# Second block: 11 of 31 convolution taps of four blocks move to the tensor engine

## The chip, the cores and the metric

One core of a Trainium2 chip runs the whole program: TensorE (PE, matrix products), VectorE (DVE), ScalarE (ACT), GpSimd (POOL) and SyncE (SP, which issues the DMAs). The metric is the device time of one execution in microseconds (us); lower is better.

## The reference

Three blocks follow each other on x of 1024 positions by 1024 columns, all in float32. The change touches only the second, and of it only the mixers:

```python
h = rmsnorm(x, norm_mix_g[l])
p = h @ w_in[l]
p_rwkv = p[..., :D_RWKV_IN]
p_rwkv = p_rwkv + (token_shift(p_rwkv) - p_rwkv) * shift_mu[l]
p_conv = p[..., D_RWKV_IN:]
y_rwkv = rwkv7_group(p_rwkv, ...)
y_conv = conformer_conv_group(p_conv, ...)
x = x + jnp.concatenate([y_rwkv, y_conv], axis=-1) @ w_out[l]
```

`conformer_conv_group` makes h = a * sigmoid(b) of two halves of 512 columns, then a causal depthwise convolution along time with 31 taps (each channel has its own 31 weights and a bias), a layer norm over the channels and a SiLU:

```python
h = u[..., :D_CONV] * jax.nn.sigmoid(u[..., D_CONV:])
h = lax.conv_general_dilated(h, conv_w, window_strides=(1,), padding=[(30, 0)], feature_group_count=D_CONV) + conv_b
```

`rwkv7_group` runs, for 8 heads of 64, a state update over time (S is 64 by 64 for each head), then a norm per head, a bonus and a gate:

```python
sa = jnp.einsum('bhvk,bhk->bhv', S, a_t)
S = S * w_t[:, :, None, :] + sa[..., :, None] * b_t[:, :, None, :] + v_t[..., :, None] * k_t[:, :, None, :]
y = jnp.einsum('bhvk,bhk->bhv', S, r_t)
```

## The kernel before

`mixers_2` does all this. Time is cut into two halves of 512 positions (`hf` 0 and 1) and the recurrence into eight units `u` of 128 positions (four a half), each of two chunks `c` of 64.

**Projections.** Every projection of 128 columns for one half is 24 matmuls of 128x128 by 128x512 (each f32 product is three products of high and low halves, L1152 to L1154), cut into eight *parts* of three. `shift_mix` and `rwkv_proj` project for the recurrence (12 a half, P[hf]) and store to DRAM; `rwkv_lora` (L[hf]) has two more. `conv_project` makes block i of the convolution for one half (C[j] with i = j % 4, hf = j // 4): generator `one` projects the gate and takes its tanh into `cvh`, `two` projects the value and multiplies. Then channels lie on partitions and time along the row, so that a tap is `h[:, j:j+512]` times one column of weights.

**Taps.** Tap 0 with the bias starts `cva` on ACT (L1496). Of the other 30, 10 are `other`: ACT multiplies into `cp` (L1500, two buffers) and POOL adds it to `cva` (L1501). 20 are `own`: DVE multiplies and adds into `cvp` (L1506, L1509), which lies in PSUM with one buffer (`cv`). A last DVE instruction adds `cvp` to `cva` (L1516). These 31 entries per block go to a list `taps`.

**The recurrence** of a unit has four generators, cut by `yield d` where d is the planner's waiting time: `rwkv_keys` (decays, normed keys), `rwkv_scores` (score matrices L1307, inverse of a triangular matrix in `chunk_inverse` by repeated products L1434 and L1441 with DVE between, L1325 and L1323 for the bonus), `rwkv_chain` (the state z through both chunks: L1352 and L1354 with z, correction rh on DVE, L1359, then `uv` copied from PSUM by DVE and ACT, L1361 and L1362, then L1365 and L1367, and z = (pc + z) * gl in two DVE instructions, L1370 and L1371) and `rwkv_post` (norm, transposes L1401, gate L1396, L1404 to L1407; result to DRAM `mixd`, for unit 7 straight into the tiles `mts1`).

**The order of the work.** PE keeps the order in which the program emits its instructions; the other engines' orders are made by the framework's scheduler from the dependences. `drive` emits: it has a clock of its own in planner units. A step of a generator costs STEP = 0.9 and is ready when its waiting time has passed; ready steps go first (chain, post, scores, keys). Otherwise one part of the list `work` is fed, which costs PART = 0.7, as long as fewer than SPARE + DENSE * steps (40 + 1.6 a step) have been fed; otherwise the clock moves by 0.25 with nothing emitted. After each turn taps are taken from the list, one for every TAP = 1.6 units. Eight units have 25 steps each.

`work` holds in order C[0], P[0], C[1], C[2], C[3], a reload with a wait of 16 units, L[1], P[1] with the norm N[0] beside it, C[4] to C[7], the load of the mixed tiles of the first half once four posts are done, a wait of 12, the first half's output projection O[0] to O[3] (64 parts, L1620 to L1622, through the small tile `xo`, two buffers, loaded at L1613 and stored at L1627) with N[1] beside it, the join of N[1], and after seven posts `mixed1` (mixed tiles of the second half), a wait of 12, and O[4] to O[7]. "Beside" means that one piece of the norm is emitted per SIDE = 4 parts; the join emits the rest, one per 2.5 units. `conv_norm` (N[hf]) first empties the taps' list, four per piece, then has two transposes (L1533) and four output pieces (L1547 to L1553, tile `cu`, stored to `mixd`) for each quarter. Ahead of `drive`, 14 projections are fed with a tap per two parts.

Of the kernel before, what the change touches and what calls it, by code (L numbers as in the profile page):

```python
# [23 lines left out]
NPART = 8  # L24
EARLY = 16
OTHER = 10
# [2 lines left out]
PART = 0.7  # L29
LOAD = 4.0  # L30
TAP = 1.6
SPARE = 40
DENSE = 1.6


# [9 lines left out]
class Kern:  # L45
# [1293 lines left out]
    def rwkv_chain(self, st, z, pool, psum):  # L1339


        nc = self.nc
        ar, sb, bkt, uv, yf, w1, gl, bon = st
        hps = [slice(0, 64), slice(64, 128)]
        pairs = [(b, h, hp) for b in range(4) for h, hp in enumerate(hps)]
        of = lambda t, c: t.rearrange("p (b c) d -> p b c d", b=4)[:, :, c]

        yp = psum.tile([128, 2, 4, 64], F32, tag="y", name="yp")
        for c in range(2):
            pc = psum.tile([128, 2, 4, 64], F32, tag="ch", name="pc")  # L1350
# [11 lines left out]
            nc.scalar.copy(uvc[64:128, :, c, 1], pc[64:128, 1])  # L1362
            yield 1.8
            for b, h, hp in pairs:
                nc.tensor.matmul(pc[hp, 0, b], lhsT=bkt[:, h, 2 * b + c], rhs=uv[:, 2 * b + c, h], start=True, stop=True)  # L1365
            for b, h, hp in pairs:
                nc.tensor.matmul(yp[hp, c, b], lhsT=sb[:, h, 2 * b + c], rhs=uv[:, 2 * b + c, h], start=False,  # L1367
                                 stop=(c == 1 and b == 3))
# [12 lines left out]
    def rwkv_post(self, q, y, st, bon, sgd, lg, pool, psum):  # L1381
# [16 lines left out]
        for b in range(4):  # L1398
            for c in range(2):
                for hp in (slice(0, 64), slice(64, 128)):  # L1400
                    nc.tensor.matmul(ps[hp, b, c], lhsT=y[hp, 4 * c + b], rhs=self.ident[hp, hp], start=True, stop=True)  # L1401
        o = pool.tile([128, 4, 128], F32, tag="mst", name="mst", bufs=1)
        for b in range(4):
            nc.scalar.activation(out=o[:, b], in_=ps[:, b].rearrange("p c t -> p (c t)"), func=ACT.Identity,  # L1404
                                 scale=c2["ln_g"][:, b:b + 1], bias=c2["ln_b"][:, b:b + 1])
# [61 lines left out]
            nc.scalar.copy(yf[qs[2 * h], :, 32:64], ps[qs[2 * h]])  # L1467
        return yf

    def conv_project(self, i, hf, xts, pool, psum, accs, taps):  # L1470


        nc = self.nc
        w = self.a["w_in_2"][0]
        cw, cb = self.c2["conv_w"], self.c2["conv_b"]
        keep = {}

        def one():
            hl = yield (w, 2304 + i * 128)
            h = keep[0] = pool.tile([128, 542], F32, tag="cvh", name="cvh", bufs=2)  # L1480
            nc.gpsimd.tensor_copy(h[:, 0:30], self.halo[:, i])
            ps = psum.tile([128, 512], F32, tag="mm", name="mps")
            yield from self.parts(ps, hl, xts[hf])
            nc.scalar.activation(out=h[:, 30:542], in_=ps, func=ACT.Tanh, scale=0.5)

        def two():
            hl = yield (w, 1792 + i * 128)
            h = keep[0]
            v = h[:, 30:542]
            ps = psum.tile([128, 512], F32, tag="mm", name="mps")  # L1490
            yield from self.parts(ps, hl, xts[hf])
            nc.vector.scalar_tensor_tensor(out=v, in0=v, scalar=1.0, in1=ps, op0=ALU.add, op1=ALU.mult)
            if hf == 0:
                nc.gpsimd.tensor_copy(self.halo[:, i], h[:, 512:542])
            acc = pool.tile([128, 512], F32, tag="cva", name="cva", bufs=4)
            nc.scalar.activation(out=acc, in_=h[:, 0:512], func=ACT.Identity, scale=cw[:, i:i + 1], bias=cb[:, i:i + 1])  # L1496
            accs.append(acc)
            def other(j):
                t = pool.tile([128, 512], F32, tag="cy", name="cp", bufs=2)
                nc.scalar.activation(out=t, in_=h[:, j:j + 512], func=ACT.Copy, scale=cw[:, 4 * j + i:4 * j + i + 1])  # L1500
                nc.gpsimd.tensor_tensor(out=acc, in0=acc, in1=t, op=ALU.add)  # L1501

            def own(j):
                x, c = h[:, j:j + 512], cw[:, 4 * j + i:4 * j + i + 1]
                if 1 in keep:
                    nc.vector.scalar_tensor_tensor(out=keep[1], in0=x, scalar=c, in1=keep[1], op0=ALU.mult, op1=ALU.add)  # L1506
                else:
                    keep[1] = psum.tile([128, 512], F32, tag="cv", name="cvp")
                    nc.vector.tensor_scalar(out=keep[1], in0=x, scalar1=c, scalar2=None, op0=ALU.mult)  # L1509

            done = 0
            for j in range(1, 31):
                mine = done < j * OTHER // 30
                done += mine
                taps.append(lambda f=other if mine else own, j=j: f(j))
            taps.append(lambda: nc.vector.tensor_tensor(out=acc, in0=acc, in1=keep[1], op=ALU.add))  # L1516
        return [one(), two()]

    def conv_norm(self, accs, taps, hf, store, pool, psum):
# [36 lines left out]
    def mixers_2(self, xt0, psum, late, es):  # L1556
# [13 lines left out]
        states, taps = {}, []  # L1570
        accs, loras, done = [[], []], [{}, {}], []
        def reload():
            yield None
# [27 lines left out]
        def out_part(hf, c0):  # L1601
# [6 lines left out]
            for t in range(4):  # L1608
                ps = psum.tile([128, 512], F32, tag="mm", name="mps")[:, :256]
                if hf == 0:  # L1610
                    x = lo.tile([128, 256], F32, tag="xo", name="xo", bufs=2)
                    xr = self.xd[t * 128:(t + 1) * 128, c0:c0 + 256]
                    nc.sync.dma_start(out=x, in_=xr)  # L1613
                else:
                    x = xs1[t][:, c0:c0 + 256]
# [95 lines left out]
        def scores(u):  # L1711
            states[u] = yield from self.rwkv_scores(states[u], r, psum, lambda: freed.append(u))

        def drive():

            running, begun = {}, {"keys": 0, "scores": 0, "chain": 0}
            tapped, fed, steps = 0.0, 0, 0

            def step(name):
                nonlocal steps
# [14 lines left out]
            def ready(name):  # L1737
                if name not in running or running[name][1] > clock[0]:
                    return False

                return name != "keys" or running[name][2] < 2 or len(freed) >= begun["keys"]
            while begun["chain"] < 8 or running:
                a, b, c = [begun[n] for n in ("keys", "scores", "chain")]
# [15 lines left out]
                    fed += 1  # L1759
                else:  # L1760
                    clock[0] += 0.25
                while tapped < clock[0] and taps:
                    taps.pop(0)()
                    tapped = max(tapped, clock[0] - 3 * TAP) + TAP

        more(EARLY)
        late(lambda: more(4 * NPART - EARLY))
# [17 lines left out]
        z = [r.tile([128, 4, 64], F32, tag="z", name="z", bufs=3)]  # L1785
        nc.gpsimd.memset(z[0], 0.0)

        C = [self.conv_project(j % 4, j // 4, xts, cv, psum, accs[j // 4], taps) for j in range(8)]
        N = [self.conv_norm(accs[hf], taps, hf, store, cv, psum) for hf in range(2)]
        O = [out_part(i // 4, 256 * (i % 4)) for i in range(8)]  # L1790
        work += C[0] + P[0][4:8] + C[1] + P[0][8:] + C[2] + C[3] + [reload(), ("wait", 16)] + L[1]
        work += [("beside", N[0])] + P[1] + [("join",)] + C[4] + C[5] + C[6] + C[7]
        work += [("when", lambda: len(posts) >= 4), mixed(), ("wait", 12), ("beside", N[1])] + O[:4]
        work += [("join",), ("when", lambda: len(posts) >= 7), mixed1(), ("wait", 12)] + O[4:]
        for i in range(14 * NPART):
            more(1)
            if i % 2 and taps:
                taps.pop(0)()
        with tc.manual_schedule(engines={mybir.EngineType.PE}):
            drive()  # L1800
            for part in feeder:
                clock[0] += PART if part else 0.25
        es.close()
        self.open_xtb("left")
        return mts1, xs1
# [492 lines left out]
```

## Time and profile before

| what | value |
|---|---|
| median of 3 runs | 3507.09 us (3503.11 to 3510.9) |
| the profiled execution | 3508.77 us |
| its span | 3507.1 us |
| TensorE's mean granted clock | 0.964 |

The span is what the trace covers; the execution's own time holds 1.7 us more around it. Positions are us from the span's start; the second block's mixers lie at about 1440 to 2162. A group's row gives line, engine, operation, output and inputs, shapes and count, then busy time, mean duration in ns, and idle time of the engine just before with what ended it. A matmul's duration overlaps the next one's, so the distance between starts tells PE's rate. In a list of waits the waiting instruction stands first, then whom it waited for, the total in us, how often, and the longest.

### The profile page before, as it was taken

How to read it: one execution, taken by the hardware profiler on the slowest of the kernel's cores; microseconds unless marked ns; L12 is line 12 of the kernel's file. 1: busy time of each engine (PE TensorE's matmuls, PEld its weight loads, DVE VectorE, ACT ScalarE, POOL GpSimd, SP SyncE). 2: the span in 40 equal slices, each digit the busy share in tenths (PEclk: the TensorE clock that was granted, in tenths of full speed). 3: DMA queues.
4: the chain of work that ended last, by engine and by line, in shares of the span. 5: the costliest groups of instructions: out<-in, count | busy, mean ns of one | idle time of the engine just before them, and what ended most of it. 6: DMA issues, size and time to landing. Idle time of an engine off the chain costs nothing.

```text
span 3507.1 us, 54368 instructions
## 1 busy us (share of the span) xinstructions
PE 3284.1 (94%) x22362; PEld 2664.9 (76%) x22362; DVE 2143.6 (61%) x3018; ACT 1166.5 (33%) x2259; POOL 1510.8 (43%) x1233
## 2 busy tenths in 40 slices
PE   8999898989999999996988788999999999998998
PEld 5877787867888888885766677888888887776877
DVE  7656787767766766758548753544443343687684
ACT  2322221232222222445546544211111143443561
POOL 3455653584434434576326524433333343344120
PEclk9999999999999999997998888999999999999999
DMA  5210035211111111452231224322221121111132
GB/s 194 73 53 25 25 106 180 75 47 49 48 42 50 47 48 48 149 167 94 67 93 50 72 93 143 102 72 73 66 69 47 51 84 37 43 34 40 43 109 78
DMA packets 276789, 261.97 MB, mean 75 GB/s; under 512 B 10178, under 2 KB 219694, under 8 KB 276538
## 3 DMA queue, kind: packets, MB, share of 16 engines
q1 hardware_dynamic: 276540, 258.48, 22.9%
q8 instruction: 176, 2.88, 0.3%
q14 instruction: 73, 0.60, 0.1%
HBM read 225.66 MB, written 32.78 MB: 74 GB/s over the span
## 4 chain that ended last, share of the span: by engine, by line
PE 38%; DVE 6%; issue 2%; POOL 2%; ACT 2%; DMA 2%; SPq 0%; POOLq 0%; DVEq 0%; ACTq 0%
PE mps L178 7%; PE mps L180 6%; PE mps L179 6%; PE dps L178 3%; PE dps L180 3%; PE dps L179 3%; DVE cvp L1506 1%; PE yp L2032 1%; PE tps L2023 1%; POOL hl L133 1%; PE mps L1152 1%; PE mps L1620 1%; DVE om L2013 1%; PE mps L1621 0%; PE mps L1622 0%
## 5 line engine op out<-in xcount | busy, mean ns | idle before, releaser
L133 POOL TENSOR_TENSOR hl<-raw,hl 128x1024 fp32r<-128x1024 f32 x249 | 629.9, 2531 | 869.3 <-ACT hl L132 661.5
L178 PE MATMUL mps<-xt,hl 128*128 128x512 f32 x1888 | 756.0, 401 | 12.7 <-DVE cacc L944 7.8
L180 PE MATMUL mps<-xt,hl 128*128 128x512 f32 x1888 | 746.2, 396 | 0.0
L179 PE MATMUL mps<-xt,hl 128*128 128x512 f32 x1888 | 746.2, 395 | 0.0
L132 ACT CAST hl<-raw 128x1024 fp32r<-128x1024 f32 x262 | 274.6, 1049 | 610.8 <-PE dps L180 441.5
L178 PEld LDWEIGHTS mps<-xt,hl 128*128 128x128 f32 x1888 | 359.6, 191 | 94.5 <-DVE cacc L944 8.2
L180 PEld LDWEIGHTS mps<-xt,hl 128*128 128x128 f32 x1888 | 358.8, 190 | 79.4 <-issue 0.9
L179 PEld LDWEIGHTS mps<-xt,hl 128*128 128x128 f32 x1888 | 359.4, 190 | 75.1 <-issue 1.0
L931 DVE SCALAR_TENSOR_TENSOR cacc<-apad,cols,cacc 128x1024 f32<-128x1024 f32 x176 | 345.0, 1964 | 112.7 <-ACT cacc L925 102.1
L178 PE MATMUL dps<-hl,hid 128*128 128x512 f32 x832 | 327.2, 393 | 2.6 <-DVE x L960 2.6
L180 PE MATMUL dps<-hl,hid 128*128 128x512 f32 x832 | 326.7, 393 | 0.6 <-POOL hid L853 0.6
L179 PE MATMUL dps<-hl,hid 128*128 128x512 f32 x832 | 326.7, 393 | 0.0
L1854 DVE TENSOR_TENSOR x<-x,dps 128x512 f32<-128x512 f32 x224 | 152.7, 687 | 171.6 <-PE dps L180 171.5
L178 PEld LDWEIGHTS dps<-hl,hid 128*128 128x128 f32 x832 | 156.6, 188 | 38.2 <-DVE x L960 3.0
L180 PEld LDWEIGHTS dps<-hl,hid 128*128 128x128 f32 x832 | 156.4, 188 | 35.9 <-POOL hid L853 1.1
L179 PEld LDWEIGHTS dps<-hl,hid 128*128 128x128 f32 x832 | 156.6, 188 | 34.5
L1841 DVE TENSOR_TENSOR ftmp<-ftmp 128x512 f32<-128x512 f32 x64 | 60.6, 949 | 177.1 <-ACT ftmp L1840 177.1
L1152 PE MATMUL mps<-xt,hl 128*128 128x512 f32 x352 | 154.4, 439 | 4.2 <-ACT cs L1552 4.2
L178 PE MATMUL mps<-hl,xt 128*128 128x512 f32 (+1 forms) x368 | 137.7, 377 | 6.1 <-ACT xt L244 1.7
L1153 PE MATMUL mps<-xt,hl 128*128 128x512 f32 x352 | 142.5, 405 | 0.0
L1154 PE MATMUL mps<-xt,hl 128*128 128x512 f32 x352 | 142.5, 405 | 0.0
L179 PE MATMUL mps<-hl,xt 128*128 128x512 f32 (+1 forms) x368 | 137.2, 374 | 1.6 <-DVE hl L133 1.3
(518 smaller groups left out, 6238.1 us busy)
## 6 DMA issues: line engine op xcount, KB each, us to landing
raw<-in_w_in_dram SPq DMA_DIRECT2D x108, 512.0 KB
raw<-in_w_ff_dram SPq DMA_DIRECT2D x64, 512.0 KB
raw<-in_ffn_up_dram SPq DMA_DIRECT2D x44, 512.0 KB
raw<-in_w_out_dram SPq DMA_DIRECT2D x36, 512.0 KB
adar<-in_ada_w_dram SPq DMA_DIRECT2D x32, 512.0 KB
adar<-in_w_ada_dram SPq DMA_DIRECT2D x48, 256.0 KB
raw<-in_ffn_down_dram SPq DMA_DIRECT2D x22, 512.0 KB
xd<-x SPq DMA_DIRECT2D x16, 512.0 KB
```

The costliest lines, as they stand in the source:

```text
L132: nc.scalar.copy(hl[:, 0], raw)
L133: (low or nc.gpsimd).tensor_tensor(out=hl[:, 1], in0=raw, in1=f32(hl[:, 0]), op=ALU.subtract)
L178: self.nc.tensor.matmul(ps, lhsT=sh, rhs=mh, start=(i == 0), stop=False)
L179: self.nc.tensor.matmul(ps, lhsT=sh, rhs=ml, start=False, stop=False)
L180: self.nc.tensor.matmul(ps, lhsT=sl, rhs=mh, start=False, stop=(i == n - 1))
L931: nc.vector.scalar_tensor_tensor(out=acc, in0=pad[:, i // 3:i // 3 + 16, i % 3:i % 3 + 64], scalar=cw[:, i * 22 + j:i * 22 + j + 1], in1=a ...
L1152: nc.tensor.matmul(ps, lhsT=sh, rhs=xt[k][:, 0], start=(k == 0), stop=False)
L1153: nc.tensor.matmul(ps, lhsT=sh, rhs=xt[k][:, 1], start=False, stop=False)
L1154: nc.tensor.matmul(ps, lhsT=sl, rhs=xt[k][:, 0], start=False, stop=(k == 7))
L1506: nc.vector.scalar_tensor_tensor(out=keep[1], in0=x, scalar=c, in1=keep[1], op0=ALU.mult, op1=ALU.add)
L1841: nc.vector.tensor_tensor(out=v, in0=v, in1=v, op=ALU.mult)
L1854: nc.vector.tensor_tensor(out=xs[t][:, c], in0=xs[t][:, c], in1=ps, op=ALU.add)
```

## The change

For the second half's blocks (C[4] to C[7], `diagonal` true), taps 0 to 10 go to PE: ACT scales the identity by one column of weights (`dg`, three buffers), and a matmul with this diagonal adds the shifted row into PSUM, 11 matmuls a block in plain f32, emitted as further parts of the generator behind two yields. ACT then makes `cva` from that PSUM tile and the bias. Taps 11 to 30 stay on DVE. The first half keeps 10 taps on ACT and POOL, in a new order. In the chain, both `uv` copies go to ACT, ACT scales the old state ahead of time (`zg`), and four DVE instructions finish the state. The norm no longer empties the taps' list but waits until all blocks are summed; taps are also handed out at the same pace behind `drive`, and one per part ahead of it. The last post waits for the mixed tiles. SPARE is 60, `xo` has one buffer, and the post's output shares y's buffer.

```diff
-SPARE = 40
+SPARE = 60
...
-            nc.vector.tensor_copy(uvc[0:64, :, c, 0], pc[0:64, 1])
-            nc.scalar.copy(uvc[64:128, :, c, 1], pc[64:128, 1])
+            for h, hp in enumerate(hps):
+                nc.scalar.copy(uvc[hp, :, c, h], pc[hp, 1])
+            zg = pool.tile([128, 4, 64], F32, tag="zg", name="zg", bufs=1)
+            for b in range(4):
+                nc.scalar.activation(out=zg[:, b], in_=z[:, b], func=ACT.Copy, scale=gl[:, 2 * b + c:2 * b + c + 1])
...
-            nc.vector.tensor_tensor(out=zn, in0=pc[:, 0], in1=z, op=ALU.add)
-            nc.vector.tensor_tensor(out=zn, in0=zn, in1=of(gl[:, :, None], c).to_broadcast([128, 4, 64]), op=ALU.mult)
+            for b in range(4):
+                nc.vector.scalar_tensor_tensor(out=zn[:, b], in0=pc[:, 0, b], scalar=gl[:, 2 * b + c:2 * b + c + 1], in1=zg[:, b],
+                                               op0=ALU.mult, op1=ALU.add)
...
-        o = pool.tile([128, 4, 128], F32, tag="mst", name="mst", bufs=1)
+        o = pool.tile([128, 4, 128], F32, tag="y", name="mst", bufs=1)
...
+            if diagonal:
+                yield
+                yield
+                diags = []
+
+                def diag(j):
+                    diags.append(pool.tile([128, 128], F32, tag="dg", name="dg", bufs=3))
+                    nc.scalar.activation(out=diags[j], in_=self.ident, func=ACT.Copy, scale=col(j))
+                diag(0)
+                diag(1)
+                ps = psum.tile([128, 512], F32, tag="mm", name="tps")
+                for j in range(OTHER + 1):
+                    if j + 2 <= OTHER:
+                        diag(j + 2)
+                    nc.tensor.matmul(ps, lhsT=diags[j], rhs=h[:, j:j + 512], start=(j == 0), stop=(j == OTHER))
+                    if j < OTHER:
+                        yield
+            acc = pool.tile([128, 512], F32, tag="cva", name="cva", bufs=4)
+            if diagonal:
+                nc.scalar.activation(out=acc, in_=ps, func=ACT.Identity, bias=cb[:, i:i + 1])
+                mine = []
+            else:
+                nc.scalar.activation(out=acc, in_=h[:, 0:512], func=ACT.Identity, scale=col(0), bias=cb[:, i:i + 1])
+                mine = [lambda j=j: other(j) for j in range(1, OTHER + 1)]
+            accs.append(acc)
+            for j in range(OTHER + 1, 31):
+                taps.append(lambda j=j: own(j))
+                if mine and j % 2:
+                    taps.append(mine.pop(0))
+            taps.extend(mine + [total])
...
-        while taps:
-            for _ in range(min(len(taps), 4)):
-                taps.pop(0)()
+        while len(summed) < 4 * (hf + 1):
             yield
...
-                    x = lo.tile([128, 256], F32, tag="xo", name="xo", bufs=2)
+                    x = lo.tile([128, 256], F32, tag="xo", name="xo", bufs=1)
...
+        def tap():
+            while tapped[0] < clock[0] and taps:
+                taps.pop(0)()
+                tapped[0] = max(tapped[0], clock[0] - 3 * TAP) + TAP
...
+                if name == "post" and begun["chain"] == 8 and len(mts1) < 8:
+                    return False
...
-        for i in range(14 * NPART):
+        while len(done) < 12:
             more(1)
-            if i % 2 and taps:
+            if taps:
                 taps.pop(0)()
         with tc.manual_schedule(engines={mybir.EngineType.PE}):
             drive()
             for part in feeder:
                 clock[0] += PART if part else 0.25
+                tap()
```

`own(j)` is as before; `total` is the last DVE instruction of a block, and appends the block to `summed`.

More of the change, by code (lines that the diff above doesn't have):

```diff
@@ L1468, in chunk_inverse, with conv_project @@
         return yf
-    def conv_project(self, i, hf, xts, pool, psum, accs, taps):
+    def conv_project(self, i, hf, xts, pool, psum, accs, taps, summed, diagonal):
         nc = self.nc
@@ L1494, in two, with own @@
                 nc.gpsimd.tensor_copy(self.halo[:, i], h[:, 512:542])
-            acc = pool.tile([128, 512], F32, tag="cva", name="cva", bufs=4)
-            nc.scalar.activation(out=acc, in_=h[:, 0:512], func=ACT.Identity, scale=cw[:, i:i + 1], bias=cb[:, i:i + 1])
-            accs.append(acc)
+            col = lambda j: cw[:, 4 * j + i:4 * j + i + 1]
+            def own(j):
+                x = h[:, j:j + 512]
+                if 1 in keep:
+                    nc.vector.scalar_tensor_tensor(out=keep[1], in0=x, scalar=col(j), in1=keep[1], op0=ALU.mult, op1=ALU.add)
+                else:
+                    keep[1] = psum.tile([128, 512], F32, tag="cv", name="cvp")
+                    nc.vector.tensor_scalar(out=keep[1], in0=x, scalar1=col(j), scalar2=None, op0=ALU.mult)
@@ L1498, in other @@
             def other(j):
                 t = pool.tile([128, 512], F32, tag="cy", name="cp", bufs=2)
-                nc.scalar.activation(out=t, in_=h[:, j:j + 512], func=ACT.Copy, scale=cw[:, 4 * j + i:4 * j + i + 1])
+                nc.scalar.activation(out=t, in_=h[:, j:j + 512], func=ACT.Copy, scale=col(j))
                 nc.gpsimd.tensor_tensor(out=acc, in0=acc, in1=t, op=ALU.add)
[L1503 to L1516, printed above, removed]
+            def total():
+                nc.vector.tensor_tensor(out=acc, in0=acc, in1=keep[1], op=ALU.add)
+                summed.append(i)
+            if diagonal:
[14 more added lines that the diff above has]
+                        yield
@@ new lines, in two @@
+            acc = pool.tile([128, 512], F32, tag="cva", name="cva", bufs=4)
+            if diagonal:
+                nc.scalar.activation(out=acc, in_=ps, func=ACT.Identity, bias=cb[:, i:i + 1])
+                mine = []
+            else:
+                nc.scalar.activation(out=acc, in_=h[:, 0:512], func=ACT.Identity, scale=col(0), bias=cb[:, i:i + 1])
[5 more added lines that the diff above has]
+                    taps.append(mine.pop(0))
@@ L1517, in conv_project, with conv_norm @@
+            taps.extend(mine + [total])
         return [one(), two()]
-    def conv_norm(self, accs, taps, hf, store, pool, psum):
+    def conv_norm(self, accs, summed, hf, store, pool, psum):
         nc, c2 = self.nc, self.c2
-        while taps:
-            for _ in range(min(len(taps), 4)):
-                taps.pop(0)()
+        while len(summed) < 4 * (hf + 1):
             yield
@@ L1568, in store @@
             nc.sync.dma_start(out=mixd[k * 128:(k + 1) * 128, hf * 512 + q * 256:hf * 512 + q * 256 + 256], in_=m)
-        states, taps = {}, []
+        states, taps, summed = {}, [], []
         accs, loras, done = [[], []], [{}, {}], []
@@ L1712, in scores @@
             states[u] = yield from self.rwkv_scores(states[u], r, psum, lambda: freed.append(u))
+        tapped = [0.0]
+        def tap():
+            while tapped[0] < clock[0] and taps:
+                taps.pop(0)()
+                tapped[0] = max(tapped[0], clock[0] - 3 * TAP) + TAP
         def drive():
             running, begun = {}, {"keys": 0, "scores": 0, "chain": 0}
-            tapped, fed, steps = 0.0, 0, 0
+            fed, steps = 0, 0
             def step(name):
@@ L1761, in drive @@
                     clock[0] += 0.25
-                while tapped < clock[0] and taps:
-                    taps.pop(0)()
-                    tapped = max(tapped, clock[0] - 3 * TAP) + TAP
+                tap()
         more(EARLY)
@@ L1786, in mixers_2 @@
         nc.gpsimd.memset(z[0], 0.0)
-        C = [self.conv_project(j % 4, j // 4, xts, cv, psum, accs[j // 4], taps) for j in range(8)]
-        N = [self.conv_norm(accs[hf], taps, hf, store, cv, psum) for hf in range(2)]
+        C = [self.conv_project(j % 4, j // 4, xts, cv, psum, accs[j // 4], taps, summed, j > 3) for j in range(8)]
+        N = [self.conv_norm(accs[hf], summed, hf, store, cv, psum) for hf in range(2)]
         O = [out_part(i // 4, 256 * (i % 4)) for i in range(8)]
@@ L1802, in mixers_2 @@
                 clock[0] += PART if part else 0.25
+                tap()
         es.close()
```

## The prediction

> **What bounds the kernel now.** I read the page first, then the second block's stretch by windows, then its waits, then single lines.
>
> ```profile
> span 3507.1 us, 54368 instructions
> PE 3284.1 (94%) x22362; PEld 2664.9 (76%) x22362; DVE 2143.6 (61%) x3018; ACT 1166.5 (33%) x2259; POOL 1510.8 (43%) x1233
> ```
>
> TensorE (PE) bounds the kernel as a whole (94%), so work that is added to it must find holes. The holes are in the stretch where the four edited convolution blocks lie. The columns: stretch and its length, busy time and instruction count of PE, weight loads, DVE, ACT and POOL, then the granted clock.
>
> ```profile
> 1843.00:1986.00 143.00, 108.22 (x1843) 86.26 (x1843) 118.93 (x198) 84.92 (x207) 97.12 (x76) 0.79 0.19 59
> 1986.00:2036.00 50.00, 47.77 (x1064) 43.16 (x1060) 27.75 (x58) 21.46 (x66) 15.89 (x11) 1.00 0.28 90
> 2036.00:2080.00 44.00, 41.12 (x1006) 36.15 (x1006) 25.37 (x55) 19.61 (x62) 14.43 (x13) 0.98 0.30 95
> 2080.00:2120.00 40.00, 21.69 (x239) 17.73 (x238) 15.12 (x31) 19.68 (x68) 12.11 (x17) 0.59 0.40 139
> ```
>
> Call these A, B, C and T. A begins where the second projection of C[4] ends; B, C and T where the chains of units 5, 6 and 7 begin. In A, PE stands idle for 143 - 108.2 = 34.8 us, and at a clock of 0.79 it loses about 108.2 x 0.21 = 22.7 us more: 57 us of slack. DVE is 83% busy there and POOL 68%. B and C are nearly full. T has 18.3 us of idleness and some 9 us (21.69 x 0.41) of slow clock. Whom PE waits for in A (total us, times, longest):
>
> ```profile
> PE ps L1441 <- DVE iq L1436: 10.5, 5, 6.0
> PE ps L1434 <- DVE ix L1443: 7.1, 3, 3.0
> PE ps L1396 <- DVE bon L1325: 4.4, 1, 4.4
> PE pc L1365 <- ACT uv L1362: 4.2, 1, 4.2
> ```
>
> These are steps of the recurrence; their DVE results come late because taps stand before them in DVE's queue. The taps by line (busy us, mean ns), over both halves, and then the first and the last DVE instruction of the second half's four blocks:
>
> ```profile
> L1506 DVE SCALAR_TENSOR_TENSOR cvp<-cvh,cols,cvp 128x512 f32<-128x512 f32 x152 | 113.9, 749 | 3.1
> L1501 POOL TENSOR_TENSOR cva<-cva,cp 128x512 f32<-128x512 f32 x80 | 106.7, 1333 | 7.3 <-ACT cp L1500 4.4
> L1500 ACT ACTIVATE cp<-cvh,cols 128x512 f32<-128x512 f32 x80 | 56.0, 719 | 27.7 <-POOL cva L1501 27.7
> ```
> ```profile
> 1842.32 0.74 DVE L1509 TENSOR_SCALAR cvp<-cvh,cols 128x512 f32<-128x512 f32 x1
> ...
> 1977.08 0.69 DVE L1516 TENSOR_TENSOR cva<-cva,cvp 128x512 f32<-128x512 f32 x1 [3.47 <-POOL cva L1501]
> ```
>
> In these 135 us the planner's clock passes about 78 units (57 parts of 0.7, some 42 steps of 0.9), enough to hand out 49 entries of the taps' list at one per 1.6 units. All 124 (31 a block) ran: DVE, ACT and POOL take taps as soon as their data exist, and only PE keeps the written order. So A holds 80 DVE taps and 40 of ACT and POOL.
>
> **The change part by part.**
>
> *Diagonal matmuls, added to PE:* 4 x 11 = 44, of 128x128 by 128x512 in plain f32. L1323 has that form; the other two rows are the same matmul of two neighbouring projection parts.
>
> ```profile
> 1668.04 1.13 PE L1323 MATMUL ps<-a,b 128*128 128x512 f32 x2
> 1669.00 0.60 PE L1263 MATMUL ps<-ident,rb 128*128 128x128 f32 x4
> ```
> ```profile
> 1561.48 0.39 PE L1152 MATMUL mps<-xt,hl 128*128 128x512 f32 x1
> 1562.16 0.39 PE L1152 MATMUL mps<-xt,hl 128*128 128x512 f32 x1
> ```
>
> What follows L1323 starts 0.96 us after it: 44 x 0.96 = +42 us of PE. A projection part (three matmuls, split into high and low halves) takes 0.68, so 0.227 a matmul, and the lower bound is 44 x 0.227 = 10 us. I take 0.96, from the row with the same operand type. By the Trainium skill ("TensorE: Matmul & The Clock Gate", Back-to-back issue gap) a matmul of 512 columns takes 518 warm cycles, about 216 ns, with no word of the type; by that the 44 would be an estimated 9.5 us. The projections agree with it and the f32 row (0.96 us) doesn't.
>
> *ACT and POOL taps of the four blocks, removed:* 40 x 1.333 = 53 us of POOL and 40 x 0.719 = 29 us of ACT go, and 44 diagonals come to ACT, 128x128 like L1230 (quoted below): 44 x 0.396 = 17 us. Neither engine sets the end, so by itself this is zero; its worth is in A's waits.
>
> *DVE taps:* the same 80, but spread. C[5]'s can't start before C[4]'s sum (one "cv" buffer), nor that before C[4]'s diagonals, and C[5]'s projections stand behind those in PE's order. By the slots counted next, C[4]'s, C[5]'s and a good half of C[6]'s taps stay in A; some 28 (28 x 0.749 = 21 us) move to B.
>
> *Part slots.* Behind A's start, before has 48 projection parts and 64 output parts. After has 96 (84 for three blocks of 16 projection parts, one empty part and 11 diagonals, and 12 for C[4]), the mixed load, then the 64. How many slots the planner opens hangs on its constants, not on the work. Before used 57 in A (48 + 18/2) and lost about 9 to the 12-unit wait behind C[7]; B and C by L1620 alone, two per part, a few records missing:
>
> ```profile
> 1843.00:1986.00 143.00, 5.39 (x18) 3.42 (x18) 0.79 0.19 59
> 1986.00:2036.00 50.00, 20.94 (x68) 12.86 (x68) 1.00 0.28 90
> 2036.00:2080.00 44.00, 13.60 (x43) 7.91 (x42) 0.98 0.30 95
> ```
>
> So after gets A 66, B about 36, C about 30 (its end was empty), unit 7's chain about 13, less 8 for the wait, which now falls into C: 137 of 161. Some 22 to 24 output parts are left when the last chain ends, where before had none. I use 22.
>
> *The stages.* Four output parts take 3.06 us:
>
> ```profile
> 2029.54 0.38 PE L1620 MATMUL mps<-hl,xt 128*128 128x256 f32 x1
> ...
> 2032.60 0.69 PE L1465 MATMUL ps<-yf,iq 32*32 32x32 f32 x32
> ```
>
> A: PE gets 33 diagonals (+32), loses 16 projection parts (-11) and 9 output parts at 0.77 (-7): +14 us of work into 57 us of slack. If the slack goes with the taps, 28 of 80 take 20 us of it along; for the 40 POOL adds and their ACT halves I let another 14 go. That is 14 - 34 = -20, between +8 (only 6 us of slack goes) and -40 (all but 3 goes). B: equal work, but 21 us of taps on a DVE that was busy 27.75 of 50: +5 (0 to 12). C: output parts to its end: +4. Unit 7's chain: 13 x 0.77 = 10 us of parts in a sparsely filled 13 us: +3.
>
> *The tail.* The last post waits for the mixed tiles, and these for all output parts and the end of the norm N[1]:
>
> ```profile
> 2092.86 0.64 PE L1367 MATMUL yp<-uv,sb 128*64 128x64 f32 x16
> ```
> ```profile
> 2099.01 0.43 DVE L1553 SCALAR_TENSOR_TENSOR cu<-cs,cu 128x256 f32<-128x256 f32 x1 [0.63 <-ACT cs L1552]
> ...
> 2103.27 0.43 DVE L1553 SCALAR_TENSOR_TENSOR cu<-cs,cu 128x256 f32<-128x256 f32 x1 [1.07 <-ACT cs L1552]
> ```
> ```profile
> 2103.73 1.90 DMA mixd<-cu
> ...
> 2107.03 7.43 DMA xt<-mixd
> ```
> ```profile
> SPq L1613 <- DMA xd<-xo: 26.0, 14, 3.2
> ```
>
> Before, unit 7's last matmuls end at 2093.5 and the mixed tiles have landed at 2114.5: 21 us. After: 22 x 0.77 = 17 us of parts; about four pieces of N[1], which advances one piece per four parts and starts late, at 4.26 us each (2103.27 - 2099.01): 17; from the last store to the landing 2114.5 - 2103.7 = 10.7. That is 45, so +24 (+7 if N[1] keeps pace). The single "xo" buffer lets each load wait for the store just ahead of it in SP's queue, 26.0 / 14 = 1.9 us, beside a load of like length: some 4.5 us per tile against 3.06 of PE, and behind the load in SP's queue stand weight loads. Five tiles are bare: 0 to +7, I take +2. Tail: +26.
>
> *At nothing.*
>
> ```profile
> L1230 ACT ACTIVATE sq<-ink,cols 128x128 f32<-128x128 f32 x32 | 10.2, 396 | 6.5 <-DMA ink<-rkvd 6.5
> ...
> L1266 DVE SCALAR_TENSOR_TENSOR kk<-ink,cols,ps 128x128 f32<-128x128 f32 x32 | 8.9, 338 | 4.0 <-PE ps L1263 3.9
> ```
>
> The state step's two DVE instructions become four of half L1266's size, so at most 4 x 0.338 = 1.4 us per half chunk, even if the removed two cost nothing; the gain is bounded by the 4.2 us that PE waited for uv, which stand in A's slack. Parts cover all but unit 7's two steps, and now those too; bare, two would cost under 3 us. The scaled states lie on ACT behind uv, during PE's work. "mst" in y's slot: the next y waits for a store (1.90 us) but comes eight planner units later; uncovered, 7 x 1.9 = 13 us. SPARE: by C[4], 32 + 1 + 16 + 96 = 145 parts are fed against a limit of 40 + 1.6 x 100 steps = 200; it never binds. The quicker hand-out of taps ahead of the drive and the even pace after it: taps run on their data, so zero, at most 5 us either way.
>
> Sum: -20 + 5 + 4 + 3 + 26 = **+18 us** on the profiled execution's 3508.77 (span 3507.1 and 1.7 around it): 3526.8. The median of the runs lies 1.7 lower, so **3525 us**, with 3515 to 3537 as this case's own range.
>
> **The rivals.** (1) *A recovers whole: faster.* POOL may delay DVE directly, not only through queues:
>
> ```profile
> L1281 DVE SCALAR_TENSOR_TENSOR a<-inr,cols,a x32: 336/342/2451, 1589.8 to 2010.1; 128x128 f32<-128x128 f32 x32
> ```
>
> One such instruction took 2.45 us against a median of 0.34. If the POOL adds cause most of A's waits, A gives -40 and B nothing: -40 + 0 + 4 + 3 + 23 = -10, 3497 us. It decides once A shortens by more than 37 us. Against it: C[4]'s 20 DVE taps stay in their place, and the longest waits name DVE. The Trainium skill ("SBUF — State Buffer", Who interferes with whom) says that a DVE instruction with two SBUF inputs contends with a GpSimd one that reads SBUF; the long L1281 agrees. Chance 0.25. (2) *Even:* A -32, tail +20, the rest as above: 3507 us, 0.15. (3) *ACT tied to PE: slower still.* With three "dg" buffers, 32 of the builds wait in ACT's queue for a matmul, with uv, y and the casts behind them; at 0.6 us of each on the path +19, 3544 us. For it: ACT lost 27.7 us in the same way to POOL (L1500's row). 0.13. (4) *The f32 matmuls go at the projections' rate:* 10 us for 42, 3493 us; L1323 speaks against it. 0.02. My forecast: 0.45.
>
> **How the numbers follow.** A difference of 0.2%, 7 us, is about what a measurement can tell from none. Slower 0.45 + 0.13 = 0.58, same 0.15, faster 0.25 + 0.02 = 0.27. The range reaches over (1) to (3): 3494 to 3546.
>
> **What would show it.** Diagonal matmuls 0.9 to 1 us apart; A's taps spread into B, A's clock near 0.9, the chain of unit 5 about 20 us earlier; output parts and N[1]'s pieces behind unit 7's chain, and the mixed tiles landing 10 to 25 us later. As many DVE waits in A as now, or no output parts behind unit 7, would prove the step concerned wrong.

## The result, and the profile after

The changed kernel takes 3530.48 us (median of 4 runs, 3526.86 to 3535.31), beside 3508.65 us for the kernel before. The ratio is 1.0065 with a 95% interval of 1.0046 to 1.0085: slower by 0.65%, where 3525 us was forecast. The profiled execution took 3533.67 us, against 3508.77 before. Its page, the span and the engines' busy time:

```profile
span 3532.0 us, 54607 instructions
PE 3315.4 (94%) x22450; PEld 2669.5 (76%) x22450; DVE 2133.0 (60%) x3034; ACT 1176.8 (33%) x2343; POOL 1455.9 (41%) x1193
```

The span grew by 24.9 us. PE is busy 31 us longer and POOL 55 us shorter. The forecast's stages A, B, C and the end, cut in the changed kernel's windows at the places that match (columns as before: PE, weight loads, DVE, ACT, POOL, then the granted clock):

```profile
1846.00:1960.00 114.00, 104.27 (x1806) 69.11 (x1806) 89.22 (x167) 68.03 (x204) 37.38 (x31) 0.96 0.15 44
1960.00:2015.00 55.00, 48.61 (x927) 32.52 (x928) 42.58 (x81) 30.05 (x92) 17.59 (x13) 0.91 0.20 64
2015.00:2068.00 53.00, 48.67 (x1096) 43.91 (x1091) 25.35 (x60) 22.33 (x74) 10.97 (x12) 1.00 0.20 62
2068.00:2108.00 40.00, 33.07 (x361) 30.75 (x358) 13.36 (x31) 15.68 (x56) 11.95 (x12) 0.96 0.37 116
2108.00:2141.00 33.00, 9.09 (x62) 6.62 (x60) 7.65 (x12) 8.16 (x19) 10.08 (x9) 0.62 0.54 181
```

A is full: PE is busy 104 of 114 us at a clock of 0.96, where before it was busy 108 of 143 at 0.79. B's DVE went from 27.75 to 42.58 us: the taps that moved. The last window is the price: for 33 us PE does 9 us of work. The starts of the chains of units 5, 6 and 7, unit 7's last matmuls, the matmul with which the second half's output parts have had their last long wait, and the first matmul behind the last of them, which marks the end of the mixers:

```profile
1960.24 0.68 PE L1352 MATMUL pc<-z,ar 64*64 64x64 f32 x16
...
2015.27 0.68 PE L1352 MATMUL pc<-z,ar 64*64 64x64 f32 x16
...
2067.80 0.68 PE L1352 MATMUL pc<-z,ar 64*64 64x64 f32 x16
...
2085.59 0.64 PE L1370 MATMUL yp<-uv,sb 128*64 128x64 f32 x16
...
2140.88 0.58 PE L1650 MATMUL mps<-hl,xt 128*128 128x256 f32 x1 [8.67 <-ACT xt L861]
...
2185.74 1.47 PE L237 MATMUL tps<-ident,xhat 128*128 128x128 f32 x12
```

The same rows in the kernel before (unit 7's last matmuls, at 2092.86, are shown above the result):

```profile
1985.61 0.68 PE L1352 MATMUL pc<-z,ar 64*64 64x64 f32 x16
...
2036.28 0.68 PE L1352 MATMUL pc<-z,ar 64*64 64x64 f32 x16
...
2080.38 1.12 PE L1352 MATMUL pc<-z,ar 64*64 64x64 f32 x16
...
2119.98 0.58 PE L1622 MATMUL mps<-hl,xt 128*128 128x256 f32 x1 [1.59 <-POOL xt L862]
...
2161.97 1.91 PE L237 MATMUL tps<-ident,xhat 128*128 128x128 f32 x16
```

Unit 5's chain begins 25.4 us earlier, unit 7's 12.6 us earlier, and the mixers end 23.8 us later. The recurrence was hastened, and what follows it lost more. The two longest waits of PE in A, which before were 10.5 and 7.1 us on the inverse's DVE steps alone:

```profile
PE ps L1445 <- DVE iq L1440: 6.1, 3, 3.3
PE tps L1533 <- DVE cvh L1496: 1.6, 2, 0.8
```

The end, row by row: the last output part of the first half, the norm N[1]'s last four pieces, and unit 7's post.

```profile
2108.09 0.29 PE L1652 MATMUL mps<-hl,xt 128*128 128x256 f32 x1
2108.21 0.38 PE L1577 MATMUL tps<-ident,cy 128*128 128x128 f32 x2
2109.84 0.44 PE L1577 MATMUL tps<-ident,cy 128*128 128x128 f32 x2 [1.25 <-DVE xo L1655]
2110.90 0.44 PE L1577 MATMUL tps<-ident,cy 128*128 128x128 f32 x2 [0.61 <-ACT cs L1582]
2116.23 0.69 PE L1577 MATMUL tps<-ident,cy 128*128 128x128 f32 x2 [4.90 <-ACT cs L1582]
2116.72 1.92 PE L1400 MATMUL ps<-sgd,lg 128*128 128x128 f32 x8
```

So 22 us of output parts follow unit 7's last matmuls (2086.2 to 2108.2), and behind them four bare pieces of the norm, with no output parts beside them. The norm's last transposes start at 2116.23; in the kernel before they start 20.7 us earlier, close behind unit 7's last matmuls:

```profile
2095.52 0.67 PE L1547 MATMUL tps<-ident,cy 128*128 128x128 f32 x2 [1.65 <-ACT cs L1552]
```

The tile "xo" and the loads of the mixed tiles (first and last start):

```profile
L1655 DVE TENSOR_TENSOR xo<-xo,mps x16: 420/422/422, 2030.0 to 2109.4; 128x256 f32<-128x256 f32 x16
...
  DMA xo<-xd: 22.7, 12
```
```profile
L860 SPq DMA_DIRECT2D xt<-mixd x8: 319/427/1358, 2114.9 to 2135.1; - x8
```

DVE waits 22.7 us for loads into the single "xo", which it did not do at all before, and the loads of the mixed tiles go out up to 2135, where before they went from 2094.2 to 2110.3. The chain that ended last shows the pace of the tail. Up to 2109 it goes round "xo" (store, load, add, store), and behind that it goes round the tile "cu" of the norm's pieces, which has one buffer before and after the change:

```profile
2100.58 1.81 DMA xd<-xo
2102.40 2.23 DMA xo<-xd
...
2104.76 0.42 DVE xo L1655
2105.20 1.77 DMA xd<-xo
...
2113.05 1.80 DMA mixd<-cu
...
2116.67 6.09 DMA mixd<-cu
```

From one store of "xo" to the next are 4.6 us here, and 5.2 and 6.1 in the two rounds before, so the last 18 output parts (four to a tile) go at the pace of the single buffer and not at PE's. In SP's queue two weight loads (L163, 512 KB each, issued at 2113.42 and 2115.29) stand just ahead of the "cu" store that takes 6.09 us; no run tests whether they lengthen it.

### The profile page after: what moved, and what is told of

Same layout as the page of the kernel before. It is cut to its first block, busy times and chain, and to the rows that moved or that the text cites. A ratio compares the mean times of both kernels' runs of the same rounds, so it can differ in the third digit from the quotient of the medians.

```text
span 3532.0 us, 54607 instructions
## 1 busy us (share of the span) xinstructions
PE 3315.4 (94%) x22450; PEld 2669.5 (76%) x22450; DVE 2133.0 (60%) x3034; ACT 1176.8 (33%) x2343; POOL 1455.9 (41%) x1193
## 3 DMA queue, kind: packets, MB, share of 16 engines
q1 hardware_dynamic: 276540, 258.48, 22.7%
## 4 chain that ended last, share of the span: by engine, by line
PE 62%; DVE 10%; DMA 5%; POOL 3%; ACT 3%; issue 3%; DVEq 0%; SPq 0%; POOLq 0%; ACTq 0%
PE mps L178 11%; PE mps L180 11%; PE mps L179 11%; PE dps L178 5%; PE dps L180 5%; PE dps L179 5%; PE mps L1152 2%; DVE cacc L931 2%; PE mps L1153 2%; PE mps L1154 2%; POOL hl L133 1%; DVE cvp L1504 1%; PE yp L2071 1%; DMA adar<-in_ada_w_dram 1%; DVE aacc L331 1%
```

## The experiments

The theory was the forecast's: TensorE gets 40 us of diagonals, the taps that leave ACT and POOL give stage A back, and the planner's slots for the diagonals push output parts and the norm behind unit 7's chain. The rivals: the relief comes from the recurrence's own edits; TensorE's added time costs the same wherever it stands; the single "xo" or the norm's late start makes the tail. Each run has its ratio to the kernel before with the 95% interval; where a time is given it is a median of 5 to 12 runs. The kernel before had a median of 3508 us in the first two groups (1 to 4, 5 to 8) and 3512.7 us in the third (9 to 12), so ratios are compared.

**1. All other edits without the diagonals.**

```diff
-accs[j // 4], taps, summed, j > 3) for j in range(8)]
+accs[j // 4], taps, summed, False) for j in range(8)]
```

> All other edits without the diagonals: uv and the scaled states on ScalarE, mst in y's slot, xo single, the new hand-out of taps. Theory (the second half's relief comes from the 40 taps that leave ScalarE and GpSimd, and the loss from the diagonals' slots; the rest costs nothing): within 5 us of the kernel before, 3504 to 3514 us, stage A (second projection of C[4] to unit 5's chain) 138 to 148 us, no output part behind unit 7's chain. Rival (the relief comes from the recurrence's steps, which moved off VectorE): A shorter by 10 to 27 us, 3482 to 3499 us.

3535.29 us, 1.0075 (1.0063 to 1.0087). Both were wrong: with no diagonal at all the kernel loses as much as the whole change. Stage A's length is as before (142.5 us from C[4]'s first own tap to unit 5's chain, 143.3 before), so the recurrence's edits shorten nothing there. The loss is at the end. The norm's first transposes, first and last start:

```profile
L1563 PE MATMUL ps<-ident,cva x16: 272/374/477, 2095.9 to 2115.2; 128*128 128x128 f32 x16
```

All 64 output parts are done by then, and unit 7's chain as well; before, the norm began at 2058.6, with 55 parts done. The change lets N[1] wait until the planner's clock has handed out every tap ("summed"), where before N[1] handed out the rest itself; this wait is called the new gate below, the earlier way the old one. Neither theory had named this; run 5 tests it.

**2. The taps left out.** Taps 1 to 10 of the four blocks are dropped, with their slots.

```diff
-            if diagonal:
-                yield
+            if False:
...
-                nc.scalar.activation(out=acc, in_=ps, func=ACT.Identity, bias=cb[:, i:i + 1])
+                nc.scalar.activation(out=acc, in_=h[:, 0:512], func=ACT.Identity, scale=col(0), bias=cb[:, i:i + 1])
```

> Leaves out taps 1 to 10 of the second half's four blocks: no diagonals and no parts for them, and no products and sums on ScalarE and GpSimd either. Theory: with nothing added to TensorE, A gives the 27.6 us that it gave beside the diagonals and the 14 us of PE work that it had to take in: about 41 us less than 143; no tail beyond the one before: 3465 to 3483 us. Rival (the relief was the recurrence's edits): the time of the kernel with all other edits, within 5 us. Rival (TensorE's written order alone bounds A): 3504 to 3513 us.

3507.54 us, 0.9993 (0.9984 to 1.0003): far from the theory's 3465 to 3483 and from the 3535 of the first rival. The time lies in the range of the second rival (3504 to 3513), but not for its reason, since A did shorten. The bounds of A, C[4]'s first own tap and unit 5's chain:

```profile
1846.28 0.74 DVE L1507 TENSOR_SCALAR cvp<-cvh,cols 128x512 f32<-128x512 f32 x1
```
```profile
1974.95 0.68 PE L1352 MATMUL pc<-z,ar 64*64 64x64 f32 x16
```

That is 128.7 us: without the ACT and POOL taps, and with the same PE work, A loses 14.6 us. But the mixers end only 4.2 us earlier (2157.7): in the stages behind A the output parts and the norm keep their own pace. With this gate and this "xo" it bounds the change as a whole: even if TensorE did the 11 taps in no time and without slots, it would have gained little. The new gate is in place here too, but the list is 40 entries shorter and has no slots in it, and the norm begins at 2044.3.

**3. Diagonals for two of the four blocks.**

```diff
-accs[j // 4], taps, summed, j > 3) for j in range(8)]
+accs[j // 4], taps, summed, j in (4, 5)) for j in range(8)]
```

> Diagonals for C[4] and C[5] alone, C[6] and C[7] as before. Theory: 22 diagonals at 0.91 us put 20 us on PE, all in A, and 20 taps of GpSimd go from A: A shorter by 8 to 16 us; 24 more slots, of which the empty end of C and the wait for posts take some 17, so 5 to 9 output parts behind unit 7's chain, tail longer by 4 to 10 us: 3498 to 3512 us. Rival (each diagonal costs its PE time whole, wherever it stands): half of the change's loss, 3517 to 3522 us.

3529.37 us, 1.0057 (1.0044 to 1.0070): slower than both had it. Unit 7's chain begins at 2071.2, 9.2 us earlier than before, but the norm at 2079.7, behind all output parts, as in run 1.

**4. Four diagonals to a slot.**

```diff
-                    if j < OTHER:
+                    if j < OTHER and j % 4 == 3:
                         yield
```

> The same 44 diagonals, four to a slot of the planner instead of one (32 slots fewer). Theory (the tail comes from the slots, which push output parts and the norm behind unit 7's chain): no more than 4 output parts behind it, the tail shorter by 18 to 30 us, of which B and C take back some 5 to 12 because the same work now stands inside them: 3506 to 3520 us. Rival (44 diagonals of PE time cost the same wherever they stand, PE being full to the end): 3526 to 3534 us.

3522.88 us, 1.0040 (1.0026 to 1.0053): between the two. With 32 slots fewer, 62 of the 64 output parts stand ahead of unit 7's chain, as the theory had it. But that chain then begins late (unit 5's already does, at 1995.6, 35 us later than in the change), and the norm's last piece is only 4 us earlier than in the change:

```profile
2096.08 0.68 PE L1352 MATMUL pc<-z,ar 64*64 64x64 f32 x16
```
```profile
2112.30 0.44 PE L1577 MATMUL tps<-ident,cy 128*128 128x128 f32 x2 [1.97 <-ACT cs L1582]
```

PE work that is taken out of the tail lengthens the stages ahead of it by almost as much.

**5. The other edits, and N[1] hands out the taps as before.** "taps" is passed to the norm as well.

```diff
         while len(summed) < 4 * (hf + 1):
-            yield
+            yield [taps.pop(0)() for _ in range(min(len(taps), 4) if hf else 0)]
```

> The kernel with all other edits and no diagonals (3535 us), but the second norm hands out the taps that are left itself, four at a step, as before the change, and starts when the list is empty; the change had let it wait until the clock had handed them out. Theory (its loss is that the norm's pieces all stand behind unit 7's chain: first piece at 2095.9 us with 64 output parts done, against 2058.6 us and 55 before): the first piece comes at 2055 to 2075 us, the last within 5 us of the chain's end, and the time falls to 3507 to 3518 us, what is left being A's 6 us. Rival (the recurrence's edits on ScalarE and the single xo buffer cost it): 3530 to 3538 us, with the norm early and the end where it was.

3514.17 us, 1.0018 (1.0010 to 1.0027), as the theory had it. The gate alone made 0.57% of run 1's 0.75%, about 20 us. The norm begins where it did before the change:

```profile
L1563 PE MATMUL ps<-ident,cva x16: 271/272/473, 2059.0 to 2085.9; 128*128 128x128 f32 x16
```

**6. The change with that gate.** The same edit, in the changed kernel.

> The changed kernel with the same old gate of the second norm. Its norm began at 2058.8 us with 25 output parts done, so here the slots, not the gate, hold it late; the gate moves it some 12 output parts ahead and three of the five pieces that stand bare behind the last output part go beside parts. Theory: 3518 to 3527 us. Rival (the norm's late pieces are the whole tail): below 3514 us. Rival (only PE's added time counts): 3527 to 3533 us.

3525.85 us, 1.0047 (1.0033 to 1.0061): within the theory's range, but not told apart from the change itself (1.0046 to 1.0085). The norm begins 13.7 us earlier (2045.0) and the mixers end 7.6 us earlier (2178.2). The list is shorter here (21 entries a block instead of 31), which may be why the gate holds the norm back less than in run 1.

**7. Two blocks with that gate.**

> Diagonals for C[4] and C[5] alone and the old gate. With the new gate the norm began at 2079.7 us, behind all output parts, and ended at 2113.6, while unit 7's chain began 9 us earlier than in the kernel before. Theory (the gate ate the gain): the norm ends with unit 7's chain at about 2092, 3496 to 3511 us. Rival (the 20 us of diagonals stay in the total): 3518 to 3530 us.

3517.77 us, 1.0025 (1.0015 to 1.0035): 11 us better than run 3, worse than expected by 7, and just under the rival's lower end. The norm's last piece ended at 2101.1 and not at 2092, unit 7's chain began at 2076.4, and PE still waited 5.8 us for "xo".

**8. The change with two "xo" buffers.**

```diff
-                    x = lo.tile([128, 256], F32, tag="xo", name="xo", bufs=1)
+                    x = lo.tile([128, 256], F32, tag="xo", name="xo", bufs=2)
```

> The changed kernel with two xo buffers, as before the change. Theory: the waits for xo in the tail (0.9, 0.6, 1.0, 1.1, 1.3 us) go, the norm's pieces and ScalarE take their place in part: 3523 to 3530 us. Rival (load behind store in the DMA queue sets the pace of all output parts): 3512 to 3520 us.

3521.59 us, 1.0039 (1.0028 to 1.0051): beyond the theory's gain, short of the rival's. In the profile DVE no longer waits for a load into "xo" but for PE, as before the change, and the loads of the mixed tiles end 13 us earlier:

```profile
  PE mps L1652: 13.1, 10
```
```profile
L860 SPq DMA_DIRECT2D xt<-mixd x8: 319/453/905, 2102.1 to 2122.2; - x8
```

**9. The slots kept, the diagonals left out.** Taps 1 to 10 are missing, and tap 0 is made on ACT as in run 2; the planner's parts for them stay, empty.

```diff
-                for j in range(OTHER + 1):
...
-                    nc.tensor.matmul(ps, lhsT=diags[j], rhs=h[:, j:j + 512], start=(j == 0), stop=(j == OTHER))
-                    if j < OTHER:
-                        yield
+                for j in range(OTHER):
+                    yield
...
```

> Leaves out taps 0 to 10 of the second half's four blocks (tap 0 alone is kept): no diagonals, no matmuls for them, no products on ScalarE and GpSimd, but the planner's parts for them stay, empty. It differs from the kernel with those taps left out (3507.5 us) by the parts alone, and from the change by 44 matmuls and their builds. Theory S (the parts cost by themselves, as they push some 22 output parts and the second norm behind unit 7's chain): 3518 to 3528 us. Theory P (the tail's length is TensorE's added 40 us come to the surface; empty parts only move work about): 3503 to 3512 us.

3531.41 us, 1.0056 (1.0044 to 1.0069): 3 us above theory S, in a group whose kernel before is 4 us slower. This is the change's own time, without one diagonal. It decides between the theories: against run 2 (0.9993), which differs by the empty parts alone, the slots cost 0.63%, about 22 us, with the new gate and the single "xo" in place. Against the change (1.0065) the 44 matmuls and their builds cost nothing that can be measured: by the two intervals, from 5 us less to 11 us more. Stage A runs from C[4]'s first own tap to unit 5's chain; the two rows here, and the first of them in the change:

```profile
1850.62 0.74 DVE L1507 TENSOR_SCALAR cvp<-cvh,cols 128x512 f32<-128x512 f32 x1
...
1959.93 1.12 PE L1352 MATMUL pc<-z,ar 64*64 64x64 f32 x16
```
```profile
1846.90 0.74 DVE L1507 TENSOR_SCALAR cvp<-cvh,cols 128x512 f32<-128x512 f32 x1
```

A's window, where the change has 104.27 us of PE at a clock of 0.96:

```profile
1846.00:1960.00 114.00, 86.31 (x1752) 68.12 (x1752) 85.92 (x166) 59.44 (x178) 36.77 (x32) 0.81 0.15 44
```

In clocked work that is 86.31 x 0.81 = 70 us against 104.27 x 0.96 = 100: the diagonals put 30 us into the same 114 us. The loads of the mixed tiles are as late as in the change:

```profile
L860 SPq DMA_DIRECT2D xt<-mixd x8: 319/499/1252, 2118.8 to 2137.7; - x8
```

**10. The other edits with the old gate and two "xo".** Runs 5 and 8 together, no diagonals.

> All other edits without diagonals, the old gate of the second norm and two xo buffers: what is left of the change is the recurrence's edits, mst in y's slot and the hand-out of taps. Theory (these cost nothing; the 6 us left at 3514.2 were the single xo): 3506 to 3512 us. Rival (the recurrence's edits on ScalarE cost the 6 us): 3512 to 3517 us.

3516.02 us beside 3512.69 us, 1.0011 (1.0000 to 1.0023). Judged by the ratio this is the kernel before, within what a measurement can tell; in microseconds it fell into the rival's range because the kernel before was 4 us slower in this group as well. The interval still admits the 0.18% that run 5 had left, so it does not tell the two theories apart. What the recurrence's edits, the shared slot of mst, the last post's wait and the hand-out of taps cost together is at most 0.23%, 8 us.

**11. The change with the old gate and two "xo".**

> The change with the old gate and two xo buffers. The gate alone gave 4.6 us, the buffers 8.9. Theory (separate waits): the sum, 3514 to 3520 us, the 5 to 10 us left over the kernel before being the diagonals' own. Rival (both shorten the same waits of the bare tail): 3520 to 3524 us.

3515.22 us, 1.0009 (1.0000 to 1.0017). The theory's sum holds: the two take back 0.56% of 0.65%, some 20 us, though the slots are all there. But what is left is no more than in run 10, which has no diagonals, so it is not theirs. With the norm's gate and the buffer put back, moving 44 taps to TensorE is neither a gain nor a loss that can be measured; by the intervals of runs 10 and 11 it is within 6 us either way.

**12. A faster kernel.** Two blocks with diagonals, the old gate, two "xo", and N[1] a piece for every two output parts.

```diff
-                        if side and n % SIDE == 0:
+                        if side and n % (2 if side is N[1] else SIDE) == 0:
```

> Diagonals for C[4] and C[5] alone, old gate, two xo buffers, and the second norm one piece for two output parts instead of four. From 3517.8 us with the gate: its tail still shows waits for xo (5.8 us) and a norm that ends 7.7 us behind unit 7's chain. Theory (these two go, and half the diagonals stand in A's slack): 3502 to 3511 us. Rival (denser norm pieces delay the recurrence by what they save at the end): 3512 to 3518 us.

3496.29 us beside 3512.69 us, 0.9953 (0.9939 to 0.9968): faster than both kernels, and by more than expected (its profiled execution took 3487.83 us). The transposes of the norm's second step, the loads of the mixed tiles, and the two last windows of the tail:

```profile
L1577 PE MATMUL tps<-ident,cy x16: 272/273/421, 2029.4 to 2073.4; 128*128 128x128 f32 x16
```
```profile
L860 SPq DMA_DIRECT2D xt<-mixd x8: 319/320/432, 2084.5 to 2090.3; - x8
```
```profile
2068.00:2108.00 40.00, 34.72 (x443) 32.20 (x444) 13.28 (x29) 20.48 (x67) 14.24 (x12) 0.96 0.56 189
2108.00:2141.00 33.00, 31.23 (x252) 30.25 (x251) 8.97 (x18) 13.52 (x24) 21.64 (x21) 1.00 0.46 160
```

The norm has ended at 2073.5, ahead of the end of unit 7's last matmuls (2093.9), so the mixed tiles are loaded while the chain still runs, and PE goes from the chain straight into the second half's output parts: 31 of 33 us busy where the change had 9. The mixers end at 2141.2, against 2162.0 before. How much of this is owed to the two blocks' diagonals was not tried: a kernel without diagonals and with the denser norm might be as fast, or faster.

## Why the prediction was right

The time (3525 forecast, 3530 measured) and its sign were right, and the tail came about as forecast. Stage A did not: two of its terms were far off, and it was luck that they had opposite signs. The terms on the span, with the rows above:

- **A, -20 forecast:** unit 5's chain came 25.4 us earlier. Counted from C[4]'s first own tap, which starts 4.6 us later than before, A went from 143.3 to 113.3 us, -30.0. The runs part this: the ACT and POOL taps -14.6 (run 2; 14 was let go for them); the empty slots, which move own taps and output parts out of A, another -19.4 (run 9: 1850.6 to 1959.9, 109.3 us); the diagonals +4.0. The forecast charged +32 for the diagonals, and let 18 go for the parts that leave and 20 for the own taps. **The step that failed is the first one of these:** "PE gets 33 diagonals (+32)". The slack of 57 us was counted, but as something that only taps could free; the diagonals went into it by themselves. Their number was right (some 33 of 44 ran in A), and so was the time of each; the price of +32 came out as +4.0. The other two terms were too large in their turn, 38 for the 19.4 that run 9 shows, so that A as a whole missed by 10 us and not by 28.
- **B +5, C +4, unit 7's chain +3:** +4.4, +8.4 and +5.3, from the chain rows.
- **The tail, +26:** +31.0 (from unit 7's last matmuls to the end of the mixers: 99.5 us, 68.5 before). The mechanism was the one forecast: parts and late norm pieces behind the chain, the mixed tiles landing late. 22 output parts at 0.77 us, 17 us in all, were forecast to be left when the chain ends; 18 were, and took 22 us with their waits. Run 9 shows that the slots make this tail without a diagonal, while the new gate and the single "xo" are in place; run 11 has all the slots and, with both put back, hardly any loss. In the profiles of all fourteen kernels of this document the mixers end 63 to 70 us after the start of the norm's last transposes (66.4 before, 69.5 in the change), while that start moves from 2073 to 2124. The norm's end thus goes with the end of the mixers, whatever delayed it; that is a regularity and not a test of its own.
- The rest of the program: +1.1. Together -25.4 + 4.4 + 8.4 + 5.3 + 31.0 + 1.1 = 24.8, beside 24.9 for the difference of the spans (rounding).

Two terms that the forecast had small were not. **The single "xo"** was put at +2 (0 to 7), as five bare tiles of 4.5 us against 3.06; two buffers take back 0.26%, about 9 us (1 to 17 by the two intervals). The forecast had the queue's pace nearly right (4.5 us a tile, 4.6 to 6.1 measured), but not that it sets the time of all parts that are left, nor that DVE, waiting for a load, holds the norm's steps that stand behind it. PE's piece at 2109.84 waits for xo. The following ones wait for ACT, which waits for DVE, which in turn waits for the store of "cu". **The hand-out of taps** was put at nothing, since taps run on their data. It was overlooked that the edit of the hand-out makes N[1] wait for the hand-out: 20 us in a kernel without diagonals (runs 1 and 5); with them the 0.18% of run 6 lies within the intervals, and only both remedies together are told apart (run 11). SPARE does nothing, as forecast: with 40 in place of 60 the program is the same to the byte.

The rivals. *A recovers whole* decided at 37 us and A gave 30 at most; the chains did come early, and the end took it back. *Even* had A nearly right (-32), but the tail at +20 and not at +31. *ACT tied to PE*: the waits are there, and cost nothing that can be measured. The row of the builds' tile:

```profile
L1526 ACT ACTIVATE dg<-ident,cols x44: 385/401/402, 1489.3 to 2011.4; 128x128 f32<-128x128 f32 x44
...
  PE tps L1533: 17.6, 27
```

ACT stands 17.6 us behind PE in 27 of the 44 builds, which is the forecast's picture of 32 builds at 0.6 us; but run 9, with no builds, is no faster. *The f32 matmuls at the projections' rate* is refuted by the three first diagonals, and by the row that follows them:

```profile
1845.89 2.84 PE L1533 MATMUL tps<-cvh,dg 128*128 128x512 f32 x6 [0.78 <-DVE cvh L1496]
1848.57 0.60 PE L1296 MATMUL ps<-ident,inv 128*128 128x128 f32 x4
```

2.68 us for three, each recorded as two: 0.89 us a diagonal, near the 0.96 that was taken, and 3.9 times the 0.227 of a projection matmul. The Trainium skill ("FP8 and Floating Point Precision", TensorE Precision Notes) says that true FP32 makes four passes through the array; the factor of 3.9 agrees with that.

What stays open: the shares of the gate and of "xo" in the change itself are told apart only as a pair; the slots were tested without diagonals only where both were as in the change; the single "cu", whose store holds two of the norm's last pieces, was left as it is in every run; and the two blocks' diagonals in run 12 were not tested alone.

## What to carry to other kernels

Ask first which work ends the stage behind the one that is relieved: here it was a norm that goes one piece per four slots, and the slots, the gate and the buffer that delayed it together made the loss, while 40 us of added matmuls went into TensorE's holes at no price that could be measured. When a planner counts slots, a new slot can delay everything behind it in the list, even when it is empty; and an edit that only changes who hands out work must be followed to whoever waits for the hand-out.

## What the runs showed of the hardware

Where PE's holes were filled, its clock was higher: in the same 114 us of stage A the granted clock was 0.81 with empty slots and 0.96 with the diagonals in them, so 30 us of clocked work came in while the stage grew by 4. The Trainium skill ("TensorE: Matmul & The Clock Gate", HAM oscillation) says that the array falls back to the slow clock when a wait between matmuls is long enough; these two windows agree with it.

One DVE instruction of the norm took 2.15 us beside a running POOL instruction, five times the median of 0.43 us for the same form:

```profile
2108.10 4.65 POOL L133 TENSOR_TENSOR hl<-raw,hl 128x1024 fp32r<-128x1024 f32 x2 [1.92 <-ACT hl L132]
```
```profile
2110.87 2.15 DVE L1583 SCALAR_TENSOR_TENSOR cu<-cs,cu 128x256 f32<-128x256 f32 x1 [0.63 <-ACT cs L1582]
```

It ends near the POOL instructions' end (2112.75 in the records), and it stands on the path that ends the tail. It is not alone: in the fourteen profiles this line runs 112 times for the second half's norm. All 19 that took longer than 0.5 us (0.56 to 2.59) overlapped with a POOL addition or subtraction of at least 128x512. Of the 93 others (0.38 to 0.49) two did, by 0.05 and 0.21 us. No run moved the POOL instructions, so this is an observation and not a test.
